# An MLP block in fp16 Strassen form: the fifth product of the second matmul goes to the second level

## The chip, the cores and the metric

The kernel runs on one core of one Trainium2 chip. The metric is the device time of one execution in microseconds (us), lower is better. A core has five engines that run side by side, each in its own program order: PE (TensorE, matmuls; its weight loads are listed as PEld), DVE (VectorE), ACT (ScalarE), POOL (GpSimd) and SP (SyncE, which here only issues transfers). They meet through semaphores. The transfers themselves (DMA) are carried by 16 engines that all issuers share.

## The reference, cut to what matters

```python
def setup_inputs():
    batch, seq_len, hidden_dim = 8, 1024, 1024
    intermediate_dim = 4 * hidden_dim
    # x: 8 x 1024 x 1024, w1: 1024 x 4096, w2: 4096 x 1024, all float32

def reference(x, w1, w2):
    h = x @ w1
    h = 0.5 * h * (1 + np.tanh(np.sqrt(2 / np.pi) * (h + 0.044715 * h ** 3)))
    return (h @ w2).astype(np.float32)
```

Two matmuls with a GELU between them, over 8192 rows.

## The kernel before

The rows are taken in eight superblocks (SB0 to SB7) of 1024. In each, both matmuls are done in Strassen's way: the operands are cut into 2 x 2 blocks, and seven block products (M1 to M7) of sums of blocks replace eight. In the names below "21" is the block in row 2, column 1; the term tables say what each product multiplies:

```python
B_TERMS = {1: ("11", SUB, "22"), 2: ("11", None, None), 3: ("12", ADD, "22"), 4: ("21", ADD, "11"),
           5: ("22", None, None), 6: ("11", ADD, "12"), 7: ("21", ADD, "22")}      # of w1 and w2
A_TERMS = {1: ("11", "22"), 2: ("21", "22"), 3: ("11", None), 4: ("22", None),
           5: ("12", "11"), 6: ("21", "11"), 7: ("12", "22")}                      # of x and g: u - v
```

The sums of w1 and w2 are made in SB0 and SB1 and stored in DRAM as fp16; SB2 to SB7 load them. In each superblock the first matmul (16 chunks of 28 matmuls of 512 columns) fills g, the GELU's result; the second consumes it.

For SB2 to SB7 most products of the second matmul are cut once more ("second level"): an `Inner` product M has its own 2 x 2 blocks and seven inner products of half the size in each direction, with matmuls of 256 columns. Its w2 operands (`y`, seven tiles) and their sums were made earlier and lie in `in_d`; its g operands are differences `x` of blocks of g, and sums `s` of these. Before, M1, M2, M3, M6 and M7 are done so, and M4 and M5 as plain products of 64 matmuls of 512 columns.

```python
W_SUMS  = {1: (5, "12", SUB, "11"), 2: (6, "22", SUB, 1), 3: (7, "22", SUB, "12"), 4: (4, 2, SUB, "21")}
W_ORDER = (1, 6, 2, 7, 5, 4, 3)                      # order in which an Inner multiplies and loads
EARLY   = ((1, "11"), (1, "21"), (2, "11"), (2, "21"))

FILL_2 = slots("""00:x122 x112 a11 a12 a13 a14 x222 x212 x622 x612 x621 x611
    ;12:a21;14:a22;15:a23;17:a24
    ;21:u0 u1;22:a31;23:u2 u3;24:a32;25:a33 d11;26:d22;27:a34 d21 d12
    ;32:g50;34:g51 e11;35:g52 e22;36:e21;37:g53 e12
    ;50:a61 x721;51:a62 x722;52:a63 x711;53:a64 x712
    ;64:a71;66:a72;67:a73;71:a74;72:n5;73:n1;74:n2;75:n7;76:n6""")
```

`FILL_2` says which VectorE jobs stand after which step: `25:a33 d11` is, after step 5 of product 2, the sum a3 number 3 and the quarter 11 of d. x = difference of two blocks of g, a = sum of x operands, g = operand of a plain product, u and d and e = additions of results, n = an operand of the next superblock.

```python
    up = ctx.enter_context(tc.tile_pool(name="up", bufs=26))     # "u": 26 tiles of 4 KB a partition
    gcp = ctx.enter_context(tc.tile_pool(name="gcp", bufs=4))    # "gc"
    tp = ctx.enter_context(tc.tile_pool(name="tp", bufs=10))     # "tmp"
    pp = ctx.enter_context(tc.tile_pool(name="pp", bufs=8, space=bass.MemoryType.PSUM))   # "ps"
    ...
    class Inner:                                     # a product of the second level
        ...
        def multiply(self, j, bank, first):          # one of its seven: 16 matmuls of 256 columns
            t = self.x[S_TERMS[j]] if j in S_TERMS else ...        # x operand or s sum
            for i in range(2):
                for c in range(NI // 2):
                    nc.tensor.matmul(bank[:, i * OH // 2:(i + 1) * OH // 2],
                                     lhsT=t[:, c, i * P:(i + 1) * P], rhs=self.y[j][:, c, :], ...)

        def steps(self, into):                       # base is None except in the last superblock
            ...
            ab, bb, cb = psum(), psum(), psum()
            self.multiply(1, ab, True)
            v = temp()
            act_copy(v, ab)                          # ACT, into a "tmp" tile
            yield 1
            self.multiply(6, bb, True)
            tt(c12, pair(v), pair(bb), ADD, True)    # DVE; c11 .. c22 are quarters of "u" tiles
            yield 2
            self.multiply(2, ab, False)              # False: goes on adding in the same bank
            act_copy(c11, pair(ab))
            yield 3
            self.multiply(7, bb, False)
            tt(c21, pair(v), pair(bb), ADD, True)
            yield 4
            self.multiply(5, cb, True)
            tt(c22, c21, pair(cb), ADD, True)
            yield 5
            self.multiply(4, ab, True)
            tt(c21, c21, pair(ab), SUB, True)
            yield 6
            self.multiply(3, cb, False)
            tt(c12, c12, pair(cb), ADD, True)
            yield 7

    def matmul2(sb, g, early, nxt):
        u2, u = halves()                             # block 11 of the output, two "u" tiles
        ...
        def post5(q, ps):                            # after each quarter of the plain M5
            store(sb, "12", q, copy(q, ps), accum_op=ADD)   # added in DRAM to what M3 stored
            tt(u[q], u[q], ps, SUB, True)
            if not end:
                store(sb, "11", q, u[q])
        ...
        order = (4, 1, 2, 3, 5, 6, 7)
        for m, after in zip(order, order[1:] + (None,)):
            if after is not None:
                load(after)                          # transfers of the next product's w2 operands
            if m in products:
                into[m], rows[m] = halves()          # two fresh "u" tiles for the result
                for n in products[m].steps(into[m]):
                    run((m, n))                      # the VectorE jobs of FILL_2
                continue
            for q in range(NQ):
                ps = psum()
                matmuls2(ps, ..., pieces[m], True, pin=True)    # 16 matmuls of 512 columns
                posts[m](q, ps)
                run((m, q))
```

The calls marked `True` at the end, `act_copy` and the matmuls of `Inner` keep the program's order; other instructions may be placed by the scheduler, and the places of tiles in a pool are given by it too. In the first matmul of SB2, GpSimd makes the second-level sums of w2 for M1 and M3 (`split_on_pool`), and at the end of each first matmul from SB2 on it makes the four `EARLY` differences of g.

Of the kernel before, what the change touches and what calls it, by code (L numbers as in the profile page):

```python
# [14 lines left out]
P = 128  # L15
# [36 lines left out]
FROM_2 = (2,)  # L52
FROM_SUMS = (1, 3)
INNER = MADE_INNER + FROM_2 + FROM_SUMS
IN_PLACE = (6, 7)
# [9 lines left out]
W_TERMS = {1: "11", 2: "21", 3: "22"}  # L65
W_SUMS = {1: (5, "12", SUB, "11"), 2: (6, "22", SUB, 1), 3: (7, "22", SUB, "12"), 4: (4, 2, SUB, "21")}
S_TERMS = {1: "11", 2: "12", 4: "22"}
S_SUMS = {1: (5, "21", ADD, "22"), 2: (6, 1, SUB, "11"), 3: (7, "11", SUB, "21"), 4: (3, "12", SUB, 2)}
EARLY = ((1, "11"), (1, "21"), (2, "11"), (2, "21"))
W_ORDER = (1, 6, 2, 7, 5, 4, 3)  # L70


def slots(table):
    return {(int(k[0]), int(k[1])): v.split() for k, v in (row.split(":") for row in table.split(";"))}


FILL_2 = slots("""00:x122 x112 a11 a12 a13 a14 x222 x212 x622 x612 x621 x611
    ;12:a21;14:a22;15:a23;17:a24
    ;21:u0 u1;22:a31;23:u2 u3;24:a32;25:a33 d11;26:d22;27:a34 d21 d12
    ;32:g50;34:g51 e11;35:g52 e22;36:e21;37:g53 e12  # L80
    ;50:a61 x721;51:a62 x722;52:a63 x711;53:a64 x712
    ;64:a71;66:a72;67:a73;71:a74;72:n5;73:n1;74:n2;75:n7;76:n6""".replace("\n    ", ""))


@with_exitstack
def kernel(
# [51 lines left out]
    def unit(rows, cols):  # L138
        return up.tile([P, rows, cols], DT, name="u")
# [134 lines left out]
    class XOps(dict):  # L274
# [5 lines left out]

        def make(self, *ms, cols=slice(None), pin=False):
            for m in ms:
                u, v = A_TERMS[m]
                if m not in self:
                    self[m] = unit(KH, HT)
                tt(self[m][:, :, cols], self.blocks[u][:, :, cols], self.blocks[v][:, :, cols], SUB, pin)
# [72 lines left out]
    def matmul1(xs, sb, quads):  # L359
# [27 lines left out]
        xb = [None]  # L387
        early = {1: {}, 2: {}}
        blocks = None
# [27 lines left out]
        for c in range(NI):  # L417
# [36 lines left out]
            if sb < 2 and j:  # L454
                ahead(q + 1, j)
            if sb == 2 and c < 8 and c % 2 == 0:
                split_on_pool(FROM_SUMS[c // 4], c // 2 % 2)
            if 1 < sb < NSB - 1:
# [4 lines left out]
                if c > 8 and c % 2:  # L463
                    x_transpose(xb[0], load_in_order, blocks, range((c - 9) // 2, (c - 7) // 2))
            if sb > 1 and c >= NI - 4:
                m, b = EARLY[c - NI + 4]
                early[m][b] = unit(NI // 2, HT // 2)
                gu, gv = (inner_block(g[t], b) for t in A_TERMS[m])
                nc.gpsimd.tensor_tensor(out=early[m][b], in0=gu, in1=gv, op=SUB)  # L469
        finish(*late)  # L470
# [21 lines left out]
    def matmul2_made(sb, g, keep_w1, xb):  # L492
# [105 lines left out]

        fill = [lambda m=m: xs.make(m, pin=True) for m in (5, 1, 2, 7, 6)]
        if sb:  # L600
# [52 lines left out]

    def split_on_pool(m, h):

        raw = []
        for k in range(2):
            raw.append(unit(2, HALF))
            q = 2 * k + h
            nc.sync.dma_start(out=flat(raw[k]), in_=stored(w2_d[q], raw2_d[q], m))  # L660
        t = {}
        for n, (_, u, op, v) in W_SUMS.items():
            if n % 2:
                two = unit(2, HALF)
            t[n] = two[:, (n + 1) % 2]
            in0, in1 = (
                t[b] if isinstance(b, int) else raw[int(b[0]) - 1][:, int(b[1]) - 1] for b in (u, v)
            )
            nc.gpsimd.tensor_tensor(out=t[n], in0=in0, in1=in1, op=op)
            nc.gpsimd.dma_start(  # L670
                out=in_d[m][:, n - 1, h * QC:(h + 1) * QC, :].rearrange("p c n -> p (c n)"), in_=t[n]
            )

    def inner_block(t, b):
        a, k = int(b[0]) - 1, int(b[1]) - 1
        return t[:, k * NI // 2:(k + 1) * NI // 2, a * HT // 2:(a + 1) * HT // 2]

    def quarter(acc, b):
        a, o = int(b[0]) - 1, int(b[1]) - 1
        return acc[a][:, :, o * OH // 2:(o + 1) * OH // 2]  # L680
# [4 lines left out]
    class Inner:  # L685
# [49 lines left out]
        def steps(self, into):  # L735

            base = self.base
            c11, c12, c21, c22 = (quarter(into, b) for b in ("11", "12", "21", "22"))
            if base is not None:
                b11, b12, b21, b22 = (quarter(base, b) for b in ("11", "12", "21", "22"))  # L740
            ab, bb, cb = psum(), psum(), psum()
            self.multiply(1, ab, True)
            v = temp()
            act_copy(v, ab)
            yield 1
            self.multiply(6, bb, True)
            tt(c12, pair(v), pair(bb), ADD, True)
            if base is not None:
                tt(c12, c12, b12, ADD, True)
            yield 2  # L750
            self.multiply(2, ab, False)
            if base is None:
                act_copy(c11, pair(ab))
            else:
                tt(c11, b11, pair(ab), ADD, True)
            self.part("11", c11)
            yield 3
            self.multiply(7, bb, False)
            tt(c21, pair(v), pair(bb), ADD, True)
            if base is not None:  # L760
                tt(c22, c21, b22, ADD, True)
                tt(c21, c21, b21, ADD, True)
            yield 4
            self.multiply(5, cb, True)
            tt(c22, c21 if base is None else c22, pair(cb), ADD, True)
            self.part("22", c22)
            yield 5
            self.multiply(4, ab, True)
            tt(c21, c21, pair(ab), SUB, True)
            self.part("21", c21)  # L770
            self.rows(1, into[1])
            yield 6
            self.multiply(3, cb, False)
            tt(c12, c12, pair(cb), ADD, True)
            self.part("12", c12)
            self.rows(0, into[0])
            yield 7

# [41 lines left out]
    def matmul2(sb, g, early, nxt):  # L820
        end = sb == NSB - 1
        ops, pieces = {}, {}
        u2, u = halves()
        into, rows = {}, {}

        def out(o, **kw):
# [4 lines left out]
            2: Inner(2, g, out("21", accum_op=ADD), x=early[2]),  # L831
            3: Inner(3, g, out("12")),
            6: Inner(6, g, out("22", accum_op=ADD)),
        }
# [4 lines left out]

        def copy(q, ps):  # L840
            t = temp()
            act_copy(t, ps)
            return t

        def post4(q, ps):
            act_copy(u[q], ps)
            store(sb, "21", q, u[q])

        def post5(q, ps):
            store(sb, "12", q, copy(q, ps), accum_op=ADD)  # L850
            tt(u[q], u[q], ps, SUB, True)
            if not end:
                store(sb, "11", q, u[q])

        posts = {4: post4, 5: post5}

        def load(m):
            if m in products:
                products[m].load()
            else:  # L860
                pieces[m] = load_pieces(m)

        def run(key):
            for job in FILL_2.get(key, ()):
                kind, m, i = job[0], int(job[1]), job[2:]
                if kind == "x":
                    products[m].make_x(i)
                elif kind == "a":
                    products[m].make(int(i))
                elif kind == "g":  # L870
                    ops[m, int(i)] = operand2(g, m, int(i), True)
                elif kind == "u":
                    tt(u[m], u[m], rows[1][m], ADD, True)
                elif kind in "de":
                    b = job[1:]
                    d = quarter(into[1], b)
                    tt(d, d, quarter(into[2 if kind == "d" else 3], b), SUB if kind == "d" else ADD, True)
                    if job in ("e21", "e12"):
                        a = int(b[0]) - 1
                        store_rows(sb, "22", a, into[1][a])  # L880
                elif nxt is not None:
                    nxt.make(m, pin=True)

        order = (4, 1, 2, 3, 5, 6, 7)
        load(4)
        run((0, 0))
        for m, after in zip(order, order[1:] + (None,)):
            if after is not None:
                load(after)
            if m in products:  # L890
                into[m], rows[m] = halves()
                for n in products[m].steps(into[m]):
                    run((m, n))
                continue
            for q in range(NQ):
                ps = psum()
                a = ops.get((m, q))
                matmuls2(ps, operand2(g, m, q) if a is None else a, pieces[m], True, pin=True)
                posts[m](q, ps)
                run((m, q))  # L900

# [46 lines left out]
```

## Time and profile before

| what | before |
|---|---|
| median of 3 runs (lowest to highest) | 1527.99 us (1527.71 to 1528.13) |
| span of the profiled execution | 1525.9 us, 22990 instructions |
| PE busy | 1517.1 us (99%) |
| DVE busy | 1073.8 us (70%) |
| ACT busy | 486.3 us (32%) |
| POOL busy | 357.2 us (23%) |
| granted TensorE clock | 0.999 |
| transfers | 417.84 MB, 274 GB/s on average |

The page lists for each engine its busy time, the span in 40 slices, the transfer queues, the chain of work that ended last, and the costliest groups of instructions. In a group's line the numbers after the bar are the busy time in us, the mean duration of one instruction in ns, and the idle time of the engine just before them with what ended most of it. A matmul's listed duration is longer than the distance to the next one, since they are pipelined; the distance comes from the chain.

### The profile page before, as it was taken

Reading aid. Unit: us, or ns where it says so; the run is one execution under the profiler, and the core shown is the slowest. Engines: PE = TensorE matmul, PEld = TensorE weight load, DVE = VectorE, ACT = ScalarE, POOL = GpSimd, SP = SyncE. Lnnn points to the kernel's source line nnn. Section 1 sums busy time; section 2 is a strip of 40 time slices with the busy share of each in tenths; the row PEclk is TensorE's granted clock in tenths of the full one; section 3 lists DMA queues with packets and bytes.
Section 4 is the critical chain, followed back from the end, with each engine's and each line's share of the span. In section 5 each row is a group of like instructions: output and inputs, shape, how many; then the busy total and the mean of one; then the engine's idle time right before and its main releaser. Section 6 shows DMA issues by size and latency. Waiting matters only on the chain.

```text
span 1525.9 us, 22990 instructions
## 1 busy us (share of the span) xinstructions
PE 1517.1 (99%) x8702; PEld 852.3 (56%) x8702; DVE 1073.8 (70%) x1354; ACT 486.3 (32%) x817; POOL 357.2 (23%) x380
## 2 busy tenths in 40 slices
PE   9999999999999999999999999999999999999999
PEld 4444444444444677446764477544875448744486
DVE  5876868768755787557875587656876567855786
ACT  6655024410144212442124411344113441144300
POOL 1242011211297022130212203131121400204011
PEclk9999999999999999999999999999999999999999
DMA  9999985894998899769996699966999769993697
GB/s 317 348 327 349 253 281 184 281 304 156 351 362 232 309 324 312 240 159 328 321 305 212 176 348 320 312 186 198 329 308 325 185 211 320 306 353 90 221 326 185
DMA packets 226191, 417.84 MB, mean 274 GB/s; under 512 B 78752, under 2 KB 85920, under 8 KB 225184
## 3 DMA queue, kind: packets, MB, share of 16 engines
q1 hardware_dynamic: 193536, 314.64, 61.4%
q0 software_dynamic: 32544, 101.73, 24.4%
q8 instruction: 68, 1.11, 0.3%
q14 instruction: 43, 0.35, 0.1%
HBM read 311.43 MB, written 119.54 MB: 282 GB/s over the span
## 4 chain that ended last, share of the span: by engine, by line
PE 85%; DVE 0%; issue 0%
PE ps L366 44%; PE ps L726 24%; PE ps L791 17%; DVE u L142 0%
## 5 line engine op out<-in xcount | busy, mean ns | idle before, releaser
L366 PE MATMUL ps<-u 128*128 128x512 f16 x3584 | 776.1, 379 | 3.6 <-DVE tmp L142 1.5
L366 PEld LDWEIGHTS <-u 128*128 128x128 f16 x3584 | 350.5, 98 | 427.1 <-issue 4.7
L142 DVE TENSOR_TENSOR tmp<-tmp,ps 128x512 f32<-128x512 f32 x528 | 361.7, 686 | 298.1 <-ACT tmp L430 114.6
L376 ACT ACTIVATE g<-tmp 128x512 f16<-128x512 f32 x256 | 161.1, 630 | 294.4 <-DVE tmp L142 294.3
L726 PE MATMUL ps<-u,gc 128*128 128x256 f16 x1920 | 224.3, 273 | 0.0
L142 DVE TENSOR_TENSOR u<-u 128x2048 f16<-128x2048 f16 (+3 forms) x233 | 211.9, 937 | 16.6 <-ACT u L321 11.7
L791 PE MATMUL ps<-u,gc 128*128 128x512 f16 x1024 | 222.6, 379 | 0.0
L726 PEld LDWEIGHTS <-gc 128*128 128x128 f16 x1920 | 187.9, 98 | 21.7
L376 ACT ACTIVATE g<-ps 128x512 f16<-128x512 f32 x256 | 151.4, 596 | 88.1 <-PE ps L366 87.9
L791 PEld LDWEIGHTS <-gc 128*128 128x128 f16 x1024 | 100.1, 98 | 119.6
L791 PE MATMUL ps<-u,g 128*128 128x512 f16 x640 | 139.8, 379 | 0.0
L490 POOL DMA_DIRECT2D out_dram<-u x58 | 58.5, 1019 | 311.2 <-DVE u L142 299.0
L142 DVE TENSOR_TENSOR u<-u,ps 128x512 f32<-128x512 f32 x131 | 89.7, 685 | 46.1 <-PE ps L791 17.0
L158 ACT COPY tmp<-ps 128x512 f32<-128x512 f32 x54 | 31.6, 585 | 272.1 <-PE ps L726 161.3
L469 POOL TENSOR_TENSOR u<-g,g 128x2048 f16<-128x2048 f16 x24 | 97.2, 4067 | 75.0 <-ACT g L376 60.1
L791 PEld LDWEIGHTS <-g 128*128 128x128 f16 x640 | 62.7, 98 | 75.5
L726 PE MATMUL ps<-u,g 128*128 128x256 f16 x864 | 103.1, 273 | 0.0
L478 POOL DMA_DIRECT2D out_dram<-u x52 | 39.0, 770 | 249.0 <-ACT u L158 227.3
L430 ACT COPY tmp<-ps 128x512 f32<-128x512 f32 x128 | 72.9, 569 | 69.7 <-PE ps L366 69.7
L142 DVE TENSOR_TENSOR tmp<-ps,tmp 128x512 f32<-128x512 f32 x128 | 88.3, 690 | 5.9 <-PE ps L366 1.2
L726 PEld LDWEIGHTS <-g 128*128 128x128 f16 x864 | 84.5, 98 | 11.1
L142 DVE TENSOR_TENSOR u<-tmp,ps 128x512 f32<-128x512 f32 x60 | 41.3, 688 | 63.9 <-PE ps L726 41.4
(42 smaller groups left out, 736.2 us busy)
## 6 DMA issues: line engine op xcount, KB each, us to landing
u<-w_d SPq DMA_DIRECT2D x384, 256.0 KB, 7.2
u<-in_d SPq DMA_DIRECT2D x120, 512.0 KB, 7.3
u<-raw_d SPq DMA_DIRECT2D x132, 256.0 KB, 6.6
out_dram<-u POOLq DMA_DIRECT2D x58, 512.0 KB, 9.0
u<-raw_d SPq DMA_DIRECT2D x56, 512.0 KB, 7.1
gc<-in_w_dram SPq DMA_DIRECT2D x48, 512.0 KB, 6.5
w_d<-u POOLq DMA_DIRECT2D x36, 512.0 KB, 4.2
raw_d<-u SPq DMA_DIRECT2D x32, 512.0 KB, 9.9
```

The costliest lines, as they stand in the source:

```text
L142: i = nc.vector.tensor_tensor(out=out, in0=in0, in1=in1, op=op)
L158: tc.keep_in_program_order(nc.scalar.copy(out=out, in_=in_))
L366: nc.tensor.matmul(bank, lhsT=ops[:, k, :], rhs=xs[m][:, k, :], start=(first and k == 0), stop=(k == KH - 1), skip_group_check=not first,)
L376: gelu_last[0] = nc.scalar.activation(out=g[b][:, c, :], in_=src, func=GELU)
L430: nc.scalar.copy(out=v, in_=pb)
L469: nc.gpsimd.tensor_tensor(out=early[m][b], in0=gu, in1=gv, op=SUB)
L478: return nc.gpsimd.dma_start(out=out2[r0:r0 + P, o0:o0 + OH], in_=src, **kw)
L490: return nc.gpsimd.dma_start(out=rows, in_=src, **kw)
L726: tc.keep_in_program_order(nc.tensor.matmul(bank[:, i * OH // 2:(i + 1) * OH // 2], lhsT=t[:, c, i * P:(i + 1) * P], rhs=self.y[j][:, c, : ...
L791: i = nc.tensor.matmul(pair(bank), lhsT=a[:, c, :], rhs=chunks(pieces[c // QC])[:, :, c % QC, :], start=(first and c == 0), stop=(c == NI ...
```

## The change

M5 of the second matmul goes to the second level too, in SB2 to SB7. For that its w2 sums must lie in DRAM before SB2's second matmul; VectorE makes them during SB2's first matmul, beside GpSimd's for M1 and M3. The steps of every inner product are written anew: the results that several blocks share now go on growing in one PSUM bank (a), and ScalarE copies the bank into the result's quarters as it stands after the inner products 1, 6, 7 and 4; VectorE then adds the other two banks' results. Block 12 of the output is no longer stored by M3 and added to in DRAM by M5: M3's result waits on the chip, M5's is added, and the block is stored once. Two of M6's g differences move from VectorE to GpSimd, and operands that aren't needed any more are overwritten in place (`over`), which frees tiles.

```diff
+ON_POOL = (1, 3)
+IN_M1 = (5,)
-W_SUMS = {..., 4: (4, 2, SUB, "21")}
+W_SUMS = {..., 4: (4, "21", SUB, 2)}
-EARLY = ((1, "11"), (1, "21"), (2, "11"), (2, "21"))
-W_ORDER = (1, 6, 2, 7, 5, 4, 3)
+EARLY = ((1, "11"), (1, "21"), (2, "11"), (2, "21"), (6, "11"), (6, "21"))
+W_ORDER = (1, 2, 6, 5, 7, 3, 4)
...
+FILL_2 = slots("""00:x122 x112 a11 a12 a13 a14 x222 x212 x622 x612
+    ;11:x522;13:a21;14:a22;15:a23;16:a24;17:x521
+    ;21:u0 u1;23:a31 u2;24:a32;25:a33;26:a34;27:u3 x511
+    ;31:x512;32:d11;33:a51;34:a52;35:a53;36:a54;37:d22 d21 d12
+    ;51:e11 e22;53:a61 e21;54:a62;55:a63;56:a64;57:e12 x721
+    ;61:x722 x711;62:x712 m11;63:a71;64:a72;65:a73 m22;66:a74;67:m21 m12
+    ;71:f11 f12;72:f21 f22;73:n5;74:n1;75:n2;76:n7;77:n6""")
...  (first matmul, SB2)
-            if sb == 2 and c < 8 and c % 2 == 0:
-                split_on_pool(FROM_SUMS[c // 4], c // 2 % 2)
+            if sb == 2:
+                if c < 8 and c % 2 == 0:
+                    jobs = split_in_m1(ON_POOL[c // 4], c // 2 % 2, up, "u", nc.gpsimd)
+                    while jobs:
+                        jobs.pop(0)()
+                if c in (5, 11):
+                    fill = split_in_m1(IN_M1[0], c // 11, gcp, "gc", nc.vector)
+                for _ in range({7: 1, 8: 1, 9: 1, 10: 1, 13: 2, 14: 2}.get(c, 0)):
+                    fill.pop(0)()
...  (Inner.steps)
+            a, b, c = psum(), psum(), psum()
+            for n, (j, bank, first, out, adds) in enumerate((
+                (1, a, True, "11", ()),
+                (2, b, True, None, ("11",)),
+                (6, a, False, "12", ()),
+                (5, c, True, None, ("12",)),
+                (7, a, False, "22", (("22", c),)),
+                (3, b, True, None, ("12",)),
+                (4, a, False, "21", ()),
+            ), 1):
+                self.multiply(j, bank, first)
+                if out is not None:
+                    t = quarter(into, out)
+                    if self.base is None:
+                        act_copy(t, pair(bank))
+                    else:
+                        tt(t, quarter(self.base, out), pair(bank), ADD, True)
+                for o in adds:
+                    o, ps = o if isinstance(o, tuple) else (o, bank)
+                    t = quarter(into, o)
+                    tt(t, t, pair(ps), ADD, True)
...  (matmul2)
-            3: Inner(3, g, out("12")),
-            6: Inner(6, g, out("22", accum_op=ADD)),
+            3: Inner(3, g),
+            5: Inner(5, g),
+            6: Inner(6, g, out("22", accum_op=ADD), x=early[6]),
...
-        def post5(q, ps):
-            store(sb, "12", q, copy(q, ps), accum_op=ADD)
-            tt(u[q], u[q], ps, SUB, True)
-            if not end:
-                store(sb, "11", q, u[q])
...  (jobs)
+                elif kind == "m":                    # block 11 minus M5
+                    add(u2, 5, b, SUB)
+                    if b in ("21", "12") and not end:
+                        store_rows(sb, "11", a, u2[a])
+                elif kind == "f":                    # block 12: M3 plus M5
+                    add(into[3], 5, b, ADD)
+                    if b in ("22", "12"):
+                        store_rows(sb, "12", a, into[3][a])
```

A result's tile pair `into[m]` is still taken from the 26 "u" tiles when its product begins, and the first instruction that writes it is now ScalarE's copy after step 1 of the seven.

## The prediction, made before the changed kernel had run

> **What bounds the kernel now.** I read first the busy shares and the chain that ended last, then the chain in order of time, then a table of the stages, then VectorE's timeline. The page says who sets the end:
>
> ```profile
> PE   9999999999999999999999999999999999999999
> ...
> PE 85%; DVE 0%; issue 0%
> PE ps L366 44%; PE ps L726 24%; PE ps L791 17%; DVE u L142 0%
> ```
>
> TensorE has no slice below 90%, and the chain is nothing but its three matmul lines: L366 the first matmul, L726 the second-level products, L791 the plain ones. The missing 15% is the start; the chain is traced back to 219 us. One steady superblock (SB4) of the chain in order of time, start and length in us:
>
> ```profile
> 876.93 13.81 PE ps L791 x64
> 890.74 36.68 PE ps L726 x336
> 927.42 13.81 PE ps L791 x64
> 941.24 24.45 PE ps L726 x224
> 965.69 96.69 PE ps L366 x448
> ```
>
> M4, then M1, M2, M3, then M5, then M6 and M7, then the next first matmul: each piece begins where the last ended, so TensorE waits for nothing, and a superblock is 185.45 us. The distances follow: 13.81 / 64 = 0.2158 us for 512 columns, 36.68 / 336 = 0.1092 us for 256. Next, the stages (us; busy time and count for PE, PEld, DVE, ACT, POOL; clock, DMA share, GB/s):
>
> ```profile
> 410.00:430.00 20.00, 20.00 (x94) 8.99 (x93) 13.33 (x20) 8.80 (x16) 10.36 (x12) 1.00 1.02 367
> 876.93:965.69 88.76, 88.76 (x690) 67.32 (x688) 72.92 (x82) 11.69 (x20) 16.44 (x21) 1.00 1.00 323
> 915.20:927.42 12.22, 12.22 (x113) 10.90 (x112) 10.12 (x14) 1.17 (x2) 2.33 (x2) 1.00 0.99 255
> ```
>
> The first row is the start of SB2's first matmul, the second SB4's whole second matmul, the third M3 alone. In the second matmul VectorE is 82% busy and the transfer engines are full (1.00): TensorE is the bound, with little room beside it. Last, how ScalarE and VectorE answer the inner steps of M3 (timeline: start, length, what):
>
> ```profile
> 917.04 0.59 ACT L158 COPY tmp<-ps 128x512 f32<-128x512 f32 x1 [8.20 <-PE ps L726]
> 920.47 0.58 ACT L158 COPY u<-ps 128x512 f32<-128x512 f32 x1 [2.85 <-PE ps L726]
> ...
> 883.03 1.22 DVE L142 TENSOR_TENSOR gc<-u 128x2048 f16<-128x2048 f16 x1
> 884.17 1.22 DVE L142 TENSOR_TENSOR gc<-u,gc 128x2048 f16<-128x2048 f16 x1
> ```
>
> Step 1 ends at 915.20 + 16 x 0.1092 = 916.95; the copy starts 0.09 us later, into a tmp tile, and is done at 917.63, a whole step before step 3 (918.69) touches that bank. The VectorE rows show that fp16 sums follow each other every 1.14 us; for 512-element fp32 adds it is 0.60 (starts at 914.68, 915.28, 915.88).
>
> **What the Trainium skill says.** (1) "TensorE: Matmul & The Clock Gate", Back-to-back issue gap, lists 518 cycles at 2.4 GHz for 512 columns and 262 for 256. That is 0.2158 and 0.1092 us, exactly the trace: two halves cost 1.2% more than a whole, so a second level saves less than an eighth. (2) "VectorE: DVE Perf Modes", The perf-mode tier table, gives a 2048-element bf16 tensor_tensor 1224 ns; the trace's fp16 sums take 1218 to 1228. (3) "Perfetto Trace Analysis", Matmuls, wants independent groups rotated through PSUM banks so that one's evacuation overlaps the next's matmuls. Before and after, a bank is used again two steps later, so the evacuation has one step, 1.75 us, of room. (4) "DMA: Bandwidth & Descriptors", Issuing engines are not separate DMA queues: all transfers interleave on the same 16 engines; the shares of about 1.00 agree with one common limit.
>
> **The change, part by part.**
>
> TensorE's work. M5 was 64 x 0.2158 = 13.81 us and becomes 7 x 16 = 112 matmuls x 0.1092 = 12.23: 1.58 us less, in six superblocks **9.5 us**. Nothing else on TensorE changes, so 1528.0 - 9.5 = 1518.5 us is the floor.
>
> VectorE, counted in the instruction order of both built programs: 12 more 2048-element fp16 sums (24 more, less the 12 given to GpSimd) x 1.22 = 14.6; 18 more 512-element fp32 adds x 0.69 = 12.3; 8 of 1024 for the w2 split x 0.717 (before's mean of that shape) = 5.7. Together 32.6 us, 27 of it in six second matmuls: 4.5 each, so 77 of 87 us. Beside TensorE in the sum, but the margin shrinks.
>
> ScalarE: 57 more copies x 0.585 = 33 us, on an engine 32% busy. GpSimd: 12 more sums x 4.07 = 49 us, two a superblock, with the four others at the end of the first matmul, 6 x 4.07 = 24 us in six chunks of 6.04. Hidden.
>
> Transfers, a superblock: M5's w2 operands are 3.5 MB instead of 2, and 1 MB of additions in DRAM goes. About even; at 323 GB/s 1.5 MB is 4.9 us. The first loads of the next first matmul are the tight ones, and they are asked for no later than before. I expect no wait there.
>
> The waits are where I put the gain. The tile that ScalarE's first copy writes is a fresh "u" tile; before, it was a tmp tile, of which there were enough. I looked up in the built program whose place each result tile takes.
>
> - *M3's first result tile* stands where the second w2 operand of M3 itself stood, which step 2 reads. So the copy of step 1 can't start before step 2 ends. But step 3 goes on in the same bank and needs the copy done: 0.09 to start, 0.59 to copy, some 0.17 to start matmuls again (the difference of a 256-column matmul's listed 273 ns and its distance of 109) = **0.85 us** of TensorE.
> - *M5's first result tile* stands where M2's stood, which is last read by the job d12, the last VectorE job of M3. VectorE's list there: x512 must wait for step 3 of M3 (its tile was that step's w2 operand), until 3 x 1.75 + 0.85 + 0.2 = 6.3 us after M3's start. Then come five sums x 1.135 (x512, a51 to a54) and eight adds x 0.60 (four of results, d11, d22, d21, d12) = 10.5, so d12 is done at 16.9. The copy ends at 17.5, matmuls go on at 17.6. Step 3 of M5 is due at 12.23 + 0.85 + 2 x 1.75 = 16.6. **About 1.0 us**.
>
> Both in SB2 to SB6 (in SB7, which loads nothing for a next one, the tiles stand elsewhere): 5 x 1.85 = **9.2 us**. That is the gain, given back almost to the last tenth.
>
> SB2's first matmul. The w2 split's VectorE instructions aren't kept in place, and the scheduler has put the second half far ahead of the chunk in the source: right behind the third chunk's additions, at about 427.3 us, in a queue that runs in order. Its two loads of 512 KB stand behind GpSimd's pair of loads, in the stretch with DMA share 1.02; that pair took 8.7 to 9.9 us to land from issues at 413.3 to 414.5. Issued some 2 us after them, 1 MB at 367 GB/s (2.9 us) behind 424, less what the issuers share: they land at about 427 and 430. VectorE then holds up the chunk's additions for some 3 to 4 us, of which the banks hide the rest: I take **3.0 us**, and this is the least certain term (0 to 8). The end after the last matmul stays one add and one store.
>
> Sum: 1528.0 - 9.5 + 9.2 + 3.0 = 1530.7; I say **1530.5 us**.
>
> **Rivals.**
>
> (a) *The gain arrives whole*: no wait shows, and it is 1518.5 us. For it: ScalarE is idle for 2 us and more before each copy, VectorE has 10 us free a superblock. Against: the two places of tiles above; neither is a matter of busy shares.
>
> (b) *VectorE becomes the bound of the second matmul.* At 77 of 87 us it isn't, but a wait can bunch its work, as in the M5 case. If every inner product lost 0.5 us: 6 x 6 x 0.5 = 18 us more than the floor, 1537.
>
> (c) *Transfers become the bound*: 1.5 MB more in a stage at 1.00, if the loads for the next first matmul came 5 us late six times, 30 us, 1548. Against: the additions in DRAM that go are about as dear.
>
> (d) *SB2's split blocks longer*: the loads land 5 us later than I think, 1536.
>
> **Range and chances.** The floor term is sure to 0.3 us. The M3 wait is nearly sure, the M5 wait depends on 10.5 us of VectorE work and could be 0 to 1.6 each, the split 0 to 8. The range is therefore 1523 to 1537. 2% would be 30.6 us: faster by that is below any floor, slower needs rival (c) at its worst.
>
> **What would show it.** L726's line counts 4032 matmuls (before 3360) and the plain L791 group loses 384. The distances stay 0.109 and 0.216. In the chain M5's piece is 12.2 us long, M3's has a break of 0.7 us before its step 3, and M5's one of 0.85, each with ScalarE's copy as releaser; ScalarE waits for VectorE once a superblock. In SB2's first matmul TensorE has gaps at about 428 us that end with VectorE, which itself waits for a load of a gc tile. The superblocks SB3 to SB6 take 185.45 - 1.58 + 1.85 = 185.7 us. Were SB3 to SB6 at 183.9 us, the tile waits would be wrong; were they over 187, (b) or (c) would be right; were SB2 alone longer than 190, (d).

## The result, and the profile after

The changed kernel takes **1538.72 us** (median of 4 runs, 1535.69 to 1543.48) against 1528.06 us for the kernel before, run beside it: a ratio of 1.0073 with a 95% interval of 1.0043 to 1.0102. The predicted time was 1530.5 us with a range of 1523 to 1537; the result is 8.2 us above the point and 1.7 us above the range. Its four runs lie 7.8 us apart, the kernel before's less than 1 us.

The page of the profiled execution (1536.64 us, span 1534.5 us) shows the chain's shares by engine, and the groups of the first matmul and of the second-level products (busy us, mean ns, then the idle time before them and what ended most of it):

```profile
PE 82%; DMA 2%; DVE 1%; issue 0%; ACT 0%; SPq 0%; DVEq 0%; ACTq 0%
...
L368 PE MATMUL ps<-u 128*128 128x512 f16 x3584 | 779.1, 380 | 8.7 <-DVE tmp L144 6.5
...
L738 PE MATMUL ps<-u,gc 128*128 128x256 f16 x2304 | 257.5, 273 | 7.7 <-ACT u L160 7.6
```

Before, the chain was TensorE alone. Now transfers, VectorE and ScalarE have shares in it, and the idle time has two homes. One is the second-level line L738 (its other two groups count 864 each, so the line has the 4032 matmuls foretold): 7.7 us, ended by ScalarE's copies. The other is the first matmul, L368: of its 8.7 us, 3.6 lie ahead of 219 us and were there before too; the other 5.0 are new and end with VectorE.

TensorE's timeline of SB4's second matmul shows the first home (start, length, what; in the bracket the idle time before a row and what ended it):

```profile
927.57 7.15 PE L738 MATMUL ps<-u,gc 128*128 128x256 f16 x64 [0.67 <-ACT u L160]
...
940.79 7.15 PE L738 MATMUL ps<-u,gc 128*128 128x256 f16 x64 [0.84 <-ACT u L160]
```

and ScalarE's timeline the two copies that end these waits:

```profile
926.93 0.58 ACT L160 COPY u<-ps 128x512 f32<-128x512 f32 x1 [2.91 <-PE ps L738]
...
940.16 0.59 ACT L160 COPY u<-ps 128x512 f32<-128x512 f32 x1 [3.07 <-DVE u L144]
```

These are the only two gaps between M4's end and the next first matmul. The first, 0.67 us, stands ahead of M3's step 3: the copy of M3's step 1 starts only at 926.93, when step 2 is through, a whole step later than the copy into a tmp tile did before. The second, 0.84 us, stands ahead of M5's step 3, and this time ScalarE had itself waited for VectorE. From one first matmul to the next SB3 to SB6 take 185.70 us each.

SB2 shows the second home. First TensorE's timeline at its first matmul:

```profile
408.60 22.15 PE L368 MATMUL ps<-u 128*128 128x512 f16 x100
434.31 1.14 PE L368 MATMUL ps<-u 128*128 128x512 f16 x4 [3.55 <-DVE tmp L144]
436.85 76.89 PE L368 MATMUL ps<-u 128*128 128x512 f16 x344 [1.40 <-DVE tmp L144]
```

Two gaps, 3.55 and 1.40 us. VectorE's timeline has, just before the first one ends,

```profile
432.96 0.69 DVE L679 TENSOR_TENSOR gc<-gc 128x1024 f16<-128x1024 f16 x1 [5.80 <-DMA gc<-raw_d]
```

so VectorE waited 5.80 us for the split's load, in front of the chunk's additions. L679 is the line of w2's split sums on either engine. The view of that line in this stretch gives their number and their shortest, median and longest duration in ns:

```profile
L679 POOL TENSOR_TENSOR u<-u x4: 2113/2146/2562, 430.5 to 439.2; 128x1024 f16<-128x1024 f16 x4
L679 DVE TENSOR_TENSOR gc<-gc x4: 693/1714/2681, 433.0 to 439.2; 128x1024 f16<-128x1024 f16 x4
```

Here is a thing that I hadn't reckoned with: of VectorE's four equal sums only the first takes 0.69 us. The three that start while GpSimd makes a sum take 1.42, 2.00 and 2.68.

Last, a table of stretches (us; busy time and count of PE, PEld, DVE, ACT, POOL; clock, DMA share, GB/s), the first two rows for those shown of before, and then the ten us around the gap:

```profile
410.00:430.00 20.00, 19.87 (x93) 8.86 (x91) 13.11 (x21) 8.48 (x15) 4.96 (x10) 1.00 1.03 388
885.13:974.14 89.01, 87.50 (x738) 72.01 (x736) 75.37 (x87) 16.96 (x29) 11.51 (x14) 1.00 0.96 303
430.00:440.00 10.00, 5.05 (x16) 1.79 (x15) 7.04 (x8) 1.60 (x3) 9.20 (x7) 0.75 1.04 393
```

The start of SB2 moves 388 GB/s with every transfer engine busy (before: 367 GB/s, as full). The whole second matmul has VectorE 85% busy and TensorE idle for 1.5 us. Around the gap the granted clock is 0.75: after this pause the matmuls come at about half speed for a while (the first 8 behind the second gap take 3.57 us, for 8 x 0.2158 = 1.73 at full speed). SB2's first matmul takes 513.74 - 408.8 = 104.9 us for 96.8 before, 8.1 more: 4.95 of gaps, about 2.5 of slower matmuls behind them (76.89 - 344 x 0.2158, less the 0.16 by which the last one's listed length exceeds its distance), and a small rest ahead of and between the gaps.

### The profile page after: what moved, and what is told of

The parts are those of the page before. It is cut to its first block, busy times and chain, and to the rows that moved or that the text cites. A ratio compares the mean times of both kernels' runs of the same rounds, so it can differ in the third digit from the quotient of the medians.

```text
span 1534.5 us, 23811 instructions
## 1 busy us (share of the span) xinstructions
PE 1512.0 (99%) x8990; PEld 881.2 (57%) x8990; DVE 1103.8 (72%) x1392; ACT 519.8 (34%) x874; POOL 385.8 (25%) x366
## 4 chain that ended last, share of the span: by engine, by line
PE 82%; DMA 2%; DVE 1%; issue 0%; ACT 0%; SPq 0%; DVEq 0%; ACTq 0%
PE ps L368 43%; PE ps L738 28%; PE ps L789 11%; DMA u<-raw_d 1%; DMA gc<-raw_d 1%; DVE u L144 0%; ACT u L160 0%; DMA u<-w_d 0%; DVE g L144 0%; DVE gc L144 0%; DVE gc L679 0%; DVE tmp L144 0%; SPq L669 0%; DVEq L144 0%; ACTq L160 0%
## 5 line engine op out<-in xcount | busy, mean ns | idle before, releaser
L368 PE MATMUL ps<-u 128*128 128x512 f16 x3584 | 779.1, 380 | 8.7 <-DVE tmp L144 6.5
L368 PEld LDWEIGHTS <-u 128*128 128x128 f16 x3584 | 351.2, 98 | 434.5 <-issue 13.5
L738 PE MATMUL ps<-u,gc 128*128 128x256 f16 x2304 | 257.5, 273 | 7.7 <-ACT u L160 7.6
L144 DVE TENSOR_TENSOR u<-u 128x512 f32<-128x512 f32 (+3 forms) x278 | 240.2, 898 | 15.5 <-ACT u L323 11.4
L738 PEld LDWEIGHTS <-gc 128*128 128x128 f16 x2304 | 225.4, 98 | 35.8 <-issue 9.7
L160 ACT COPY u<-ps 128x512 f32<-128x512 f32 x164 | 96.0, 585 | 419.4 <-PE ps L738 294.7
L499 POOL DMA_DIRECT2D out_dram<-u x68 | 66.6, 1201 | 403.5 <-DVE u L144 354.4
L144 DVE TENSOR_TENSOR u<-u,ps 128x512 f32<-128x512 f32 x164 | 112.1, 683 | 41.0 <-PE ps L789 16.9
L789 PE MATMUL ps<-u,gc 128*128 128x512 f16 x640 | 138.8, 379 | 0.0
L738 PE MATMUL ps<-u 128*128 128x256 f16 x864 | 99.2, 273 | 0.0
L738 PE MATMUL ps<-u,g 128*128 128x256 f16 x864 | 99.2, 273 | 0.0
L738 PEld LDWEIGHTS <-u 128*128 128x128 f16 x864 | 84.5, 98 | 11.1
L738 PEld LDWEIGHTS <-g 128*128 128x128 f16 x864 | 84.5, 98 | 9.8
L144 DVE TENSOR_TENSOR u<-g,g 128x2048 f16<-128x2048 f16 x48 | 57.5, 1221 | 44.2 <-PE ps L738 40.0
```

Of the source, the lines that this page charges most:

```text
L144: i = nc.vector.tensor_tensor(out=out, in0=in0, in1=in1, op=op)
L160: tc.keep_in_program_order(nc.scalar.copy(out=out, in_=in_))
L368: nc.tensor.matmul(bank, lhsT=ops[:, k, :], rhs=xs[m][:, k, :], start=(first and k == 0), stop=(k == KH - 1), skip_group_check=not first,)
L499: return nc.gpsimd.dma_start(out=rows, in_=src, **kw)
L738: tc.keep_in_program_order(nc.tensor.matmul(bank[:, i * OH // 2:(i + 1) * OH // 2], lhsT=t[:, c, i * P:(i + 1) * P], rhs=self.y[j][:, c, : ...
L789: i = nc.tensor.matmul(pair(bank), lhsT=a[:, c, :], rhs=chunks(pieces[c // QC])[:, :, c % QC, :], start=(first and c == 0), stop=(c == NI ...
```

## The experiments

Theory: three separate terms, the floor of -9.5 us, two tile waits of 9.2 us, and SB2's split, of which only the last was mis-sized. Rivals: the new chain form costs something everywhere, or the waits only stand in for each other. Each run was timed with the kernel before on the same chip; its ratio is to that. The medians of before were 1527.97 to 1528.35 us.

**The split alone.** The kernel before, plus `split_in_m1` for M5 in SB2 (two pairs of loads, eight VectorE sums, eight stores that nobody reads):

```diff
+            if sb == 2:
+                if c in (5, 11):
+                    fill = split_in_m1(IN_M1[0], c // 11, gcp, "gc", nc.vector)
+                for _ in range({7: 1, 8: 1, 9: 1, 10: 1, 13: 2, 14: 2}.get(c, 0)):
+                    fill.pop(0)()
```

> The kernel before, with only the w2 split of M5 by VectorE added in SB2's first matmul, its sums stored and never used; everything in the second matmul is as before. VectorE's second half stands behind the third chunk, as in the changed kernel. Theory: the whole excess of SB2 comes from this part alone: SB2's first matmul 103 to 112 us, kernel 1536 to 1543 with a spread of several us, no other stage longer. Rival (the excess needs the changed kernel's other transfers or its second matmul): SB2's first matmul under 99 us, kernel under 1531.

Measured 1540.86 us (1535.51 to 1542.08), ratio 1.0075 [1.0056, 1.0094]: this part alone costs some 12.7 us, nearly all in SB2's first matmul; the later superblocks take 185.45 us as before. Its profiled run is the longest of the four (1542.08 us). VectorE's timeline shows something there that the changed kernel's did not:

```profile
435.25 4.82 DVE L696 TENSOR_TENSOR gc<-gc 128x1024 f16<-128x1024 f16 x1 [6.64 <-DMA gc<-raw_d]
```

The first sum, too, is held up here: it takes 4.82 us, beside a pair of GpSimd's sums from 435.31 to 439.50. TensorE's gap, which ends at 440.71, is 8.52 us instead of 3.55.

**Without the loads.** The changed kernel, with the split's eight sums reading a block of x that is on chip; the four 512-KB loads are left out, and M5's w2 sums are other numbers.

```diff
-                    fill = split_in_m1(IN_M1[0], c // 11, gcp, "gc", nc.vector)
+                    fill = split_in_m1(IN_M1[0], c // 11, gcp, "gc", nc.vector, xs[3])
...
+            if engine is nc.vector:
+                raw.append(resident.rearrange("p (a k) t -> p a (k t)", a=2))
+                continue
             raw.append(pool.tile([P, 2, HALF], DT, name=name))
```

> The changed kernel, but the eight VectorE sums of the w2 split read a block of x that is on the chip already, and the four loads of 512 KB that they waited for are left out (so M5's sums are not those of w2). The sums are not kept in place and stand again early in SB2, within the first four chunks. Theory (the load's landing is the cost): SB2's first matmul 97 to 98 us, kernel 1530 to 1532. Rival (the eight sums themselves, slowed by GpSimd, are the cost): SB2's first matmul 100 us or more, kernel over 1534.

Measured 1529.04 us (1527.88 to 1530.55), ratio 1.0005 [0.9998, 1.0012]. The sums now stand at 402 to 417 us, ahead of GpSimd's first, and take 0.68 us each. SB2's first matmul takes 97.2 us, SB3 to SB6 still take 185.70 us. So without the split's loads the changed kernel is at 1529.0 us, 9.7 less. The run takes away two things at once: the loads, and the meeting of the sums with GpSimd's.

**The loads, unread.** The same, but the loads are issued as in the changed kernel; only the sums don't read them.

```diff
+            if resident is not None:     # VectorE's sums
+                src = [resident.rearrange("p (a k) t -> p a (k t)", a=2)] * 2
+            else:
+                src = raw
```

> The changed kernel with the split's loads issued as they are but not read: VectorE's sums read a resident x block (M5's w2 sums are left out of the result). If the loads cost only because a sum waits for them: 1529 us, as without the loads (1529.04), eight sums of 0.68 us, no gap at 430 us. If their two megabytes delay SB2's other loads (w1's chunks), a gap of 2 to 4 us stays where a matmul waits for a u tile's load, and the time is 1532 to 1537.

Measured 1536.73 us (1536.11 to 1536.96), ratio 1.0054 [1.0039, 1.0069]. The first line fell, the second held: with no sum reading them the 2 MB still cost 7.7 us. The view of TensorE's waits from 405 to 525 us (in total, times, longest, all us):

```profile
PE ps L368 <- DMA u<-w_d: 2.5, 2, 1.8
PE ps L793 <- DMA u<-w_d: 2.5, 4, 1.6
```

Now matmuls of the first matmul (L368) wait for w1's chunks, and then M4's (L793) for its w2 pieces, 5.0 us in all. The rest is a wait of 1.9 us for VectorE at the start, and the loads have a hand in that as well: one of the sums, at 407.34 us, waited 1.68 us for a load to land. The load isn't its operand; the sum writes into the small gc pool, whose four tiles the unread loads fill. In this kernel all four of the loads are asked for within 13 us from 399 us on, ahead of the chunks in the one queue that issues both. The stretch from 400 to 440 us is full whether they are there or not (DMA share 1.00 before, at 351 GB/s): what is added in front pushes back what follows.

**GpSimd idle.** The changed kernel with GpSimd's sums of SB2 cut to 16 of 1024 elements (the w2 sums of M1 and M3 and the `EARLY` differences are left out there; a raw block is stored in their place). The split keeps its places and its loads.

```diff
+            if engine is nc.gpsimd:
+                engine.tensor_tensor(out=t[n][:, :16], in0=raw[0][:, 0, :16], in1=raw[1][:, 0, :16], op=op)
...  (likewise for the `EARLY` differences)
```

> The changed kernel with GpSimd's sums of SB2 cut to 16 of 1024 elements (the w2 sums of M1 and M3 and the early differences are left out of the result in SB2 and what is stored is a raw block). The split's loads and its places are as in the changed kernel. If the late load is the main cause of SB2's excess in the changed kernel: the gap in PE at about 430 us stays (3.5 to 5 us and the lower clock after it), SB2's first matmul stays at 102 to 105 us and the time is 1534 to 1538. If VectorE held up by GpSimd is the main cause: the eight sums take 0.69 us each, SB2's first matmul falls to 97 to 99 us and the time to 1529 to 1532.

Measured 1537.33 us (1535.17 to 1537.74), ratio 1.0055 [1.0038, 1.0071]. TensorE's timeline (first fence) and VectorE's group of sums (second):

```profile
436.11 1.64 PE L368 MATMUL ps<-u 128*128 128x512 f16 x4 [3.48 <-DVE tmp L144]
```

```profile
L689 DVE TENSOR_TENSOR gc<-gc 128x1024 f16<-128x1024 f16 x8 | 5.5, 688 | 6.0 <-DMA gc<-raw_d 6.0
```

All eight sums are back at 0.69 us, and the second gap, at 438 us, shrinks from 1.40 to 0.49 us; the first gap stays at 3.48, for it belongs to the load. So in the places that the scheduler chose, transfers are the main cost, and GpSimd's sums a smaller one. (With its sums cut, GpSimd also issues its stores earlier; this run doesn't tell the two apart.) That smaller one is also the likely source of the spread: no run here was above 1537.8 us, and where a profile caught the first sum held up as well (the split alone, and a run below) the gap was 8.4 to 8.5 us.

**The split kept late.** VectorE's split instructions kept in the program's order, which puts them in the chunks where the source has them (7 to 10, 13 and 14) and moves the second pair of loads to 483 us.

```diff
-            engine.tensor_tensor(out=t[n], in0=in0, in1=in1, op=op)
+            i = engine.tensor_tensor(out=t[n], in0=in0, in1=in1, op=op)
+            if engine is nc.vector:
+                tc.keep_in_program_order(i)
```

> The changed kernel with one thing altered: VectorE's instructions of the w2 split of M5 are kept where the source has them, in chunks 7 to 10, 13 and 14 of SB2's first matmul, long after their loads have landed. Theory (the load of the second half, late behind other transfers, stops VectorE and with it TensorE): SB2's first matmul goes back from 104.9 us to 96.8 to 97.5, the clock there to 1.00, and the kernel to about 1530.5 us with a spread of under 1 us over its runs instead of 8. Rival (VectorE's own extra work, or sharing with GpSimd, is what costs): the work is still there, and is now all beside GpSimd's sums, so SB2's first matmul stays above 100 us.

Measured 1538.21 us (1537.27 to 1539.06), ratio 1.0065 [1.005, 1.008]: nothing gained, though no sum waits for a load any more. VectorE's and GpSimd's timelines:

```profile
496.29 8.56 DVE L679 TENSOR_TENSOR gc<-gc 128x1024 f16<-128x1024 f16 x2
```

```profile
495.51 8.06 POOL L478 TENSOR_TENSOR g<-g,g 128x2048 f16<-128x2048 f16 x2
```

Two sums that should take some 1.3 us take 8.56: the first of them ends only after both of GpSimd's `EARLY` differences, which stand back to back. A chunk's additions come behind them, and TensorE stands for 5.53 us until 505.49:

```profile
505.49 11.23 PE L368 MATMUL ps<-u 128*128 128x512 f16 x40 [5.53 <-DVE tmp L144]
```

**The split kept late, and a tile of its own.** As above, and the copy after step 1 goes into a tile of the tmp pool, which has places enough; the addition after step 2 makes the quarter from it.

```diff
-                    if self.base is None:
+                    if self.base is None and n == 1:
+                        v = temp()
+                        act_copy(v, bank)
+                    elif self.base is None:
...
-                    tt(t, t, pair(ps), ADD, True)
+                    tt(t, pair(v) if self.base is None and n == 2 else t, pair(ps), ADD, True)
```

> As e1_split_late, and ScalarE's copy after step 1 of every second-level product goes into a tmp tile again, from which VectorE's addition at step 2 makes quarter 11: same instructions, same durations. Theory (the copy waits for the place of the result tile): the waits of 0.85 us in M3 and 1.0 in M5 both go, SB3 to SB6 take 183.9 us each instead of 185.7, and the kernel comes to 1519 to 1520 us, 9 below before. Rival (VectorE or ScalarE has no room for the new steps): the waits move to another step of M3 or M5, SB3 to SB6 stay above 185 us and the kernel near 1530.

Measured 1529.01 us (1527.65 to 1531.05), ratio 1.0007 [0.9998, 1.0015]: 9.2 us less than the run above, as the two tile waits were sized. In the chain the second-level products are one piece:

```profile
896.20 73.36 PE ps L740 x672
```

672 x 0.1092 = 73.4, nothing in between, and SB3 to SB6 take 183.86 us each. What keeps this kernel from the floor is SB2.

**The split kept late, a tile of its own, GpSimd idle.** The run above with GpSimd's sums of SB2 cut as before.

> The run with the split kept late and the first copy in a tile of its own (1529.0 us), with GpSimd's sums of SB2 cut to 16 of 1024 elements (left out of the result there). Theory (in that run VectorE's eight sums are held up by GpSimd's sums and by nothing else): each of the eight takes 0.68 to 0.69 us instead of up to 5 to 8, PE's gaps in SB2 go, its granted clock stays at 1.0, SB2's first matmul takes 97 us, and the time is 1519 to 1522 us. Rival (the late split waits for its own loads or for its place in VectorE's list): sums of 0.69 us but gaps remain, and the time stays at 1526 to 1529.

Measured 1522.01 us (1520.65 to 1525.59), ratio 0.9962 [0.9947, 0.9976], 7.0 us less for GpSimd's sums alone. VectorE's group of split sums in the run above (first fence) and here (second):

```profile
L679 DVE TENSOR_TENSOR gc<-gc 128x1024 f16<-128x1024 f16 x8 | 18.8, 2361 | 0.0
```

```profile
L689 DVE TENSOR_TENSOR gc<-gc 128x1024 f16<-128x1024 f16 x8 | 5.4, 687 | 0.0
```

The same instructions at the same places: 2361 ns on the mean beside GpSimd's sums, 687 without them. For the late placing, VectorE held up by GpSimd is thus the main cause. What is left above 1520 us here is about 1.4 us in which M4 waits for its w2 pieces.

**A tile of its own alone.** The changed kernel with just the two tmp edits; the split stays where the scheduler had it.

> The changed kernel with one thing altered: the copy after step 1 goes into a PSUM-sized tile of its own (tmp) and the addition after step 2 makes the quarter from it. The split stays where it is in SB2. Theory (two tile waits of 9.2 us in all and the split's transfers in SB2 are separate terms): both waits go, SB3 to SB6 take 183.9 us each, SB2's first matmul stays at 104 to 108 us, time 1529.5 us (1526 to 1534), 9 us under the changed kernel. Rival (the waits only take up what another wait would, VectorE's list or a load): SB3 to SB6 stay above 185 us and the time at 1534 to 1539.

Measured 1533.01 us (1527.97 to 1534.27), ratio 1.0025 [1.0013, 1.0038]. SB3 to SB6 take 183.87 us each, so both waits are gone here too. The time fell by 5.7 us rather than 9.2. These runs spread over 6 us, as the changed kernel's do, and in the profiled one (1533.86 us) SB2 was the long one: SB3 begins at 608.08 us, against 602.74 in the changed kernel's profile. VectorE's timeline shows why:

```profile
435.64 5.22 DVE L679 TENSOR_TENSOR gc<-gc 128x1024 f16<-128x1024 f16 x1 [6.09 <-DMA gc<-raw_d]
```

GpSimd's pair runs from 436.11 to 440.31, and the sum ends 0.55 us after it, at 440.86; TensorE's gap is 8.38 us. In the changed kernel's profile the same sum started 0.52 us ahead of GpSimd's pair (432.96 and 433.48) and was not held up, here 0.47 us ahead, and it was. If the order of starts decides, a small shift between the two loads that the engines wait for is worth some 5 us. That would fit the spread, but no run here shows it.

**The split in SB1.** If SB2's first matmul has room neither in its transfers nor beside GpSimd, the split can move to where block 22 of w2 is on chip anyway and GpSimd only issues transfers: SB1's second matmul.

```diff
-                if c in (5, 11):
-                    fill = split_in_m1(IN_M1[0], c // 11, gcp, "gc", nc.vector)
-                for _ in range({7: 1, 8: 1, 9: 1, 10: 1, 13: 2, 14: 2}.get(c, 0)):
-                    fill.pop(0)()
...
-            fill = split_jobs(7, lambda: sums[7]) + fill + split_jobs(6, lambda: sums[6])
+            fill = split_jobs(5, lambda: pieces(5)) + split_jobs(7, lambda: sums[7]) + fill + split_jobs(6, lambda: sums[6])
...  (FILL for SB1: four more jobs; the tmp edits are in, too)
+    {(1, 2): 1, (1, 3): 1, (7, 0): 1, (7, 1): 1, ...
```

> The changed kernel with the first copy after step 1 in a tile of its own (as in the run with both), and with M5's w2 split moved from SB2 into SB1's second matmul, where block 22 of w2 is on chip and GpSimd only issues transfers. Theory (the three costs are the two tile waits, 9.2 us, and SB2's split, 8 us or more in the profiled run): both go, so SB2's first matmul takes 96.8 to 97.5 us again, SB3 to SB6 183.9 us each, and the time is 1519 us (1517 to 1522), some 9 us under the kernel before, which is the floor term alone; the spread of the runs falls below 2 us. Rival (VectorE has no room in SB1's second matmul either, or its stores there delay others): SB1 grows by what eight sums and four stores cost, 5 to 10 us, and the time is 1524 to 1529. Rival (the weight-chain form itself costs more elsewhere than the floor term says): no gain at all, 1526 to 1529, with no long wait in SB1 or SB2.

Measured 1520.3 us (1518.71 to 1521.1), ratio 0.9945 [0.9931, 0.996]. At those four blocks VectorE has already begun to turn block 22 into the sum for product 3, so that M5's w2 sums are partly other numbers in this run. The amount of work is the same. The next run puts the jobs earlier.

**The split in SB1, earlier.**

```diff
-    {(1, 2): 1, (1, 3): 1, (7, 0): 1, (7, 1): 1, ...
+    {(2, 2): 1, (2, 3): 1, (5, 0): 1, (5, 1): 1, ...
```

> The run with the split in SB1's second matmul, but with its four jobs at the blocks (2, 2), (2, 3), (5, 0) and (5, 1), so that they read block 22 of w2 before VectorE turns it into the sum of product 3 (in the run before they stood from (1, 2) on and read that sum in part; M5's w2 sums were other numbers there). The same number of instructions, nothing left out. Theory (SB1's second matmul has room on VectorE and in the transfers; the chain and the split are then both paid for): no wait in SB1 or SB2, SB3 to SB6 183.9 us each, time 1520.3 us (1518.5 to 1521.5), ratio 0.9945. Rival (at these earlier blocks VectorE has less in hand, block 22 having come just before): a gap of 2 to 6 us at the start of M5 or M1 in SB1, time 1522 to 1526.

Measured **1519.69 us** (1519.0 to 1520.74), ratio 0.9945 [0.9933, 0.9958], with nothing left out: the best version, 8.3 us faster than the kernel before and 19.0 faster than the changed one. A line of its chain, M1 to M7 of SB4 in one piece, and a stretch of its table (columns as above):

```profile
887.54 73.36 PE ps L736 x672
```

```profile
400.00:440.00 40.00, 40.00 (x186) 18.05 (x185) 26.32 (x38) 14.09 (x25) 22.76 (x26) 1.00 1.00 352
```

TensorE is busy for all of the 40 us in which the changed kernel idles for 5, the clock stays at 1.00, and the transfers are as full as ever, but with nothing new among them.

## Why the prediction was right in its terms and wrong in its sum

The runs give the sum by its terms: the best version, 1519.7, has neither waits nor the split in SB2; with the waits and without the split's loads it is 1529.0, so the waits are 9.3; the changed kernel, at 1538.7, has the split's 9.7 on top. The split's size is not one number: added to the kernel before it is 12.7, and in the kernel without the waits 13.3 (1533.0 against 1519.7).

- *The floor*, 1518.5 us: right. L738's pieces keep 0.1092 us a matmul, and SB3 to SB6 without waits take 183.86 us, 185.45 less 1.59. The best version's last matmul ends 9.15 us earlier than before's (1512.92 against 1522.07). "The end after the last matmul stays one add and one store" was 0.9 us too little: from the last matmul to the end it is 4.7 us after 3.8. Why that store takes longer I didn't test.
- *The M3 wait*, 0.85 us: right in cause and place. The gap is 0.67 us plus the restart of 0.17 that the prediction had counted in.
- *The M5 wait*, about 1.0 us: right as well, ScalarE waiting for VectorE once a superblock (in its working 6.3 + 10.5 is 16.8, not 16.9). Together they make SB3 to SB6 185.70 us each, foretold as 185.7, and giving the copy its own tile removes both (183.86).
- *VectorE not the bound*, rival (b): right for the second matmul, where it is 85% busy. *ScalarE*: 33 us more foretold, 519.8 - 486.3 = 33.5 measured. *GpSimd*: 49 us more foretold, 385.8 - 357.2 = 28.6 measured; the twelve sums do take 48.7, and its other work shrank, which the prediction had not counted. *Transfers not the bound of the second matmul*, rival (c): right; the stage moves 303 GB/s.
- *SB2's split*, "**3.0 us**, and this is the least certain term (0 to 8)": **this step failed**. The place of the sum was right (VectorE comes to it at 427.16, foretold about 427.3), and so were the gap's place and cause. The size was not. That TensorE's first gap, 3.55 us in the profile, is so near to 3.0 is luck, for two readings erred in opposite directions. "They land at about 427 and 430" was too early: I had divided 1 MB by a rate, but the queue waited for tiles and for earlier transfers, issued the second pair only from 420.69 on, and its first load landed at 432.84, so that VectorE waited 5.8 us and not 3 to 4. On the other side "the banks hide the rest" hid 2.25 us of that, more than the prediction let it. What made the term too small is what it left out. First, in a stretch whose transfer engines are full, the loads also push back others that queue behind them: unread, and all four ahead of the chunks, they made TensorE wait 5.0 us for other loads. Second, "8 of 1024 for the w2 split x 0.717" took the sums' length from stretches in which GpSimd made none: three of the eight took 1.42 to 2.68 us in this profile, which goes with a second gap of 1.40 (0.49 with GpSimd idle), and in two other runs one took 4.82 or 5.22, with a first gap of 8.4 to 8.5. Third, TensorE's clock after the gap, 2.5 us, had no term at all.
- Rival (d), the split blocking longer, is what came true, and its own sign was the right one: SB2 alone over 190 us, at 602.74 - 408.8 = 193.9. It said 1536 us for loads 5 us later than I thought; the first landed 5.8 later, and the profiled run is at 1536.64. The median lies 2 us beyond that. A VectorE held up by GpSimd, which rival (d) didn't have, is the likely reason; no profile of such a run of the changed kernel shows it.
- *The range*, 1523 to 1537: its lower end is the sum of the best cases, 1518.5 + 5 x 0.85 = 1522.8; the worst cases that the prediction names, five M5 waits of 1.6 and a split of 8, come to 1538.8 and not to 1537.

What stays open: how much of the median's 9.7 us is transfers and how much GpSimd. Without GpSimd's sums the changed kernel is 1.4 us lower, an amount within the spread of either; without the loads both are gone, because the sums then also move ahead of GpSimd's.

## What to carry to other kernels

The start of SB2, with a DMA share of 1.0, hid every transfer and yet had no room for 2 MB more: what was put in front delayed what stood behind it. So new loads belong where the data lies on chip already or where the table shows slack. Before giving VectorE an fp16 sum, look at what GpSimd does in the same microseconds, and not only at VectorE's busy share. And a result tile taken afresh from a busy pool carries the wait for whoever used its place last; putting the first copy into a tile of the tmp pool took away both waits here and brought no new one.

## What the runs showed of the hardware that I had not expected

VectorE's fp16 sums of two operands in SBUF stop while GpSimd runs a sum: 0.69 us alone, 1.42 to 5.22 beside one or two sums of 2.1 us, up to about 7.8 beside two of 4.0, ending some 0.55 us after GpSimd's does, while the fp32 additions with a PSUM operand between them keep 0.68. The Trainium skill has it, and the prediction left it out: "SBUF — State Buffer", Who interferes with whom, says that a VectorE instruction with two SBUF inputs contends with a GpSimd instruction that reads SBUF, and that the later one is blocked until the first is through. The trace agrees that VectorE is blocked entirely. The page gives the port that the two share to whichever issues first, for the whole instruction. Between two GpSimd sums in a row the runs show both outcomes: with the split kept late one VectorE sum waited through both, while in the changed kernel's profile one that started at 434.77 us, during the first, ended at 436.19 with the second under way, and that second GpSimd sum took 2.56 us for some 2.1 (the 2562 in the view above). So GpSimd can be held up as well. Nor do the recorded starts settle who waits: a sum that by the records started 0.47 us ahead of GpSimd's waited (a tile of its own alone), one 0.52 us ahead didn't (the changed kernel). Records of GpSimd are rough at that distance, so this last point is not certain.

TensorE comes back slowly from a pause. "TensorE: Matmul & The Clock Gate", What's actually happening, gives half the clock after an idle window of about 3.4 us, full again after a busy one. After the 3.55-us gap of the changed kernel the clock was 0.75 over ten us, and with unread loads, whose gaps are at most 1.89 us, it stayed at 1.00. But the run with the split kept late and a tile of its own has 0.83 over the ten us that hold a gap of 2.29 us, and 1.00 over those that hold one of 2.18, so a pause shorter than the window can be enough, and doesn't have to be.
